# Hybrid encoder block on one core: the last column group of the second token tile in two halves, its sums between the first tile's output pieces

## The chip, the cores and the metric

The kernel runs on one core of a Trainium2 chip. Five engines work side by side, each with its own queue, and meet through semaphores: TensorE (PE, matmuls; its weight loads are listed as PEld), VectorE (DVE), ScalarE (ACT), GpSimd (POOL) and SyncE (SP, which issues most DMA transfers). Matmuls write PSUM, 128 partitions with eight banks of 512 floats each; everything else lives in SBUF. The metric is the time of one execution on the device in microseconds; lower is better. An execution that is profiled also gives a span, from the first to the last instruction.

## The reference, cut to what matters

One layer (DEPTH is 1) on 256 tokens of 2048 features, all in float32:

```python
def reference(x, ...):
    u = _rms_norm(x, norm_mix_pre)
    mix = hybrid_mixer(u, ...)            # three branches, gates, w_out
    x = x + _rms_norm(mix, norm_mix_post)
    hdn = jnp.square(jax.nn.relu(_rms_norm(x, norm_mlp_pre) @ w_mlp_up))
    return x + _rms_norm(hdn @ w_mlp_down, norm_mlp_post)

def _rms_norm(x, gain):
    return x * lax.rsqrt(jnp.mean(x * x, axis=-1, keepdims=True) + 1e-6) * gain
```

The end of the kernel is the last line of the reference: the product with w_mlp_down (8192 x 2048), its norm over the 2048 features of each token, the gain and the residual. A token's norm needs all of its 2048 columns, so no column of the output can be written before the last column of the product is summed.

## The kernel before, in words

The 256 tokens are two tiles of 128 (`tt` 0 and 1). Float32 products run as products of rounded parts: a weight tile is read as `raw`, ScalarE rounds it into `whi`, VectorE subtracts to get `wlo`, and TensorE multiplies the activations' high and low parts by `whi` and their high part by `wlo`, all summed in one PSUM bank. The weights come as one stream of rows of 128 x 1024, 512 KB a piece, on SP's queue.

Most of w_mlp_down has been multiplied and added into `ys[0]` and `ys[1]` (one per token tile, 128 x 2048) when the stretch of the diff begins. What is left are the last 8 blocks of 128 hidden features (`hp`), for four column groups of 512 (`g` 0 to 3). The generator `tok` does one column group: for every pair of blocks it takes a weight tile and multiplies both token tiles by it, each into its own bank (`ps[0]`, `ps[1]`, from the pool `pg` of four banks). `lag` is the number of trailing weight tiles for which the two token tiles are parted: the first tile is finished with them, `ps[0]` is handed out, then the second is multiplied by the same tiles and `ps[1]` follows. For `g` 3 the lag is 4, all of them: 24 matmuls for the first tile, then 24 for the second (four weight tiles, two blocks each, three products a block). The three last weight tiles get buffers of their own (`spare`), so that they can stay.

As a bank is handed out, the loop at line 1574 does for that token tile: the sum into `ys` on VectorE (line 1578); the square on ScalarE, with the sum over the 512 columns accumulated into `ss4[:, tt, g]` (line 1579); for `g` 3 the mean over all columns by an activation with a bias (`rstd_of`, line 1151) and the power of -0.5 on GpSimd (line 1152), which gives `r4`; the multiplication by the gain `g4[g]` on VectorE, in place (line 1582). After `g` 2 `rstd_of` has added the sums of the first three groups and epsilon into `sum4`. Last, in five pieces of 512, 512, 512, 256 and 256 columns, VectorE writes x1 + ys * r4 into `x1` (line 1588), and each piece is sent to the output, the second and fourth on ScalarE's queue and the others on SP's (line 1589).

The end up to this stretch has its order written out by hand for TensorE, ScalarE and VectorE only in places (`tc.manual_schedule`); elsewhere, and in the loop at 1574, a scheduler orders the engines' queues by the instructions' dependencies. Instructions of one engine run in the order of its queue.

## Time and profile before

| what | value |
|---|---|
| median of three runs | 1502.87 us (1501.86 to 1506.22) |
| the profiled execution's own time | 1503.08 us |
| its span | 1501.2 us, 22710 instructions |
| mean granted TensorE clock | 0.998 |
| TensorE busy from 200 to 1100 us | 100% |
| TensorE busy from 1300 to 1400 us | 99.3% |
| HBM read and written | 279.24 MB and 2.10 MB |
| the output's ten transfers, issue to landing | 2.5 to 3.3 us each |
| GpSimd's work after the last accumulating transfer | two powers of one column |

Rows of a timeline give the start and the length in microseconds, the engine, the line of the kernel, the operation, the tile written and those read, their shapes, the count of instructions merged into the row, and in brackets the idle time before it with what ended it. Rows of groups end with the busy time, the mean of one instruction in ns, and the idle time before them. In the rows of windows the numbers after the length of the window are busy microseconds and counts of PE, PEld, DVE, ACT and POOL, then the granted clock, the share of the DMA engines and GB/s. A DMA queue's row has its packets, MB and share of 16 engines.

### The profile page before, as it was taken

The page shows a single profiled execution, that of the slowest core. Times are in us where ns is not written, and L with a number is a line of the kernel's source. Part 1 is how long each engine was busy: PE and PEld are TensorE (multiplying, and loading weights), DVE is VectorE, ACT ScalarE, POOL GpSimd, SP SyncE. Part 2 cuts the span into 40 slices and gives each one's busy share as a digit, 9 for nine tenths or more (in the row PEclk, how much of TensorE's full clock was granted, in tenths as well). Part 3 has the DMA queues.
Part 4 walks back from the last instruction along what each step waited for, and adds up shares of the span by engine and source line. Part 5 has one row for each costly group of instructions (what it writes and reads, how often), then busy time and mean ns, then how long its engine had stood idle before and what let it go on. Part 6 is the DMA issues. An engine that isn't in the chain of part 4 may idle for free.

```text
span 1501.2 us, 22710 instructions
## 1 busy us (share of the span) xinstructions
PE 1487.4 (99%) x8384; PEld 1250.2 (83%) x8384; DVE 1205.8 (80%) x1677; ACT 933.3 (62%) x1431; POOL 94.7 (6%) x151
## 2 busy tenths in 40 slices
PE   9999999999999999999999999999999999999997
PEld 8888888887788887788888888888888888888886
DVE  7965779895687895476557688998999989999996
ACT  7665677555765445564545676776666666767663
POOL 0011003000002000000000000000000000000000
PEclk9999999999999999999999999999999999999999
DMA  8655445454555455455774868889898888989874
GB/s 288 202 154 175 154 161 172 152 182 154 164 174 174 156 183 183 131 174 191 243 235 153 267 181 256 250 223 260 259 257 256 229 268 250 262 259 262 255 218 148
DMA packets 107055, 312.19 MB, mean 208 GB/s; under 512 B 12352, under 2 KB 14400, under 8 KB 106944
## 3 DMA queue, kind: packets, MB, share of 16 engines
q1 hardware_dynamic: 96336, 279.35, 57.0%
q0 software_dynamic: 8064, 29.36, 10.3%
q10 hardware_dynamic: 2544, 2.03, 0.5%
q8 instruction: 66, 1.08, 0.3%
q14 instruction: 45, 0.37, 0.1%
HBM read 279.24 MB, written 2.10 MB: 187 GB/s over the span
## 4 chain that ended last, share of the span: by engine, by line
PE 96%; DMA 1%; DVE 1%; issue 1%; ACT 1%; SPq 0%; POOLq 0%; DVEq 0%; POOL 0%; ACTq 0%
PE gps L235 28%; PE gps L191 22%; PE gps L195 12%; PE gps L220 7%; PE mps L1434 3%; PE mps L1436 3%; PE mps L1435 3%; PE gps L1436 2%; PE gps L1434 2%; PE gps L1435 2%; PE gps L197 2%; PE gps L359 1%; DMA raw<-raw 1%; PE mps L840 1%; DMA raw<-in_wst_dram 1%
## 5 line engine op out<-in xcount | busy, mean ns | idle before, releaser
L175 DVE TENSOR_TENSOR wlo<-raw,whi 128x1024 fp32r<-128x1024 f32 x570 | 691.3, 1223 | 151.0 <-ACT whi L173 140.6
L173 ACT ACTIVATE whi<-raw 128x1024 fp32r<-128x1024 f32 x570 | 597.6, 1057 | 253.7 <-PE gps L235 71.8
L191 PE MATMUL gps<-pk,whi 128*128 128x512 f32 x1460 | 370.6, 392 | 0.5 <-DVE tmp L1352 0.2
L191 PEld LDWEIGHTS gps<-pk,whi 128*128 128x128 f32 x1460 | 270.4, 188 | 56.2 <-DVE tmp L1352 1.2
L235 PE MATMUL gps<-whi,pk 128*128 128x512 f32 x1004 | 253.5, 392 | 0.0
L195 PEld LDWEIGHTS gps<-pk,wlo 128*128 128x128 f32 x1561 | 212.7, 190 | 15.2 <-DVE wlo L175 0.3
L235 PEld LDWEIGHTS gps<-whi,pk 128*128 128x128 f32 x1004 | 186.5, 188 | 40.1 <-issue 1.0
L195 PE MATMUL gps<-pk,wlo 128*128 128x256 f32 x1561 | 218.0, 282 | 0.0
L235 PE MATMUL gps<-wlo,pk 128*128 128x512 f32 x502 | 138.2, 392 | 0.0
L235 PEld LDWEIGHTS gps<-wlo,pk 128*128 128x128 f32 x502 | 93.2, 188 | 19.6 <-issue 0.2
L1434 PE MATMUL mps<-whi,fm 128*128 128x512 f32 x224 | 88.6, 396 | 1.8 <-ACT whi L173 1.7
L1351 ACT ACTIVATE tmp<-gps 128x256 f32<-128x256 f32 x64 | 24.6, 385 | 102.8 <-PE gps L197 100.9
L1435 PE MATMUL mps<-whi,fm 128*128 128x512 f32 x224 | 87.7, 392 | 0.0
L1436 PE MATMUL mps<-wlo,fm 128*128 128x512 f32 x224 | 87.4, 390 | 0.0
L1414 POOL DMA_DIRECT2D raw<-raw x56 | 48.8, 872 | 572.7 <-DVE raw L1411 299.1
L1411 DVE TENSOR_TENSOR raw<-raw,raw 128x1024 f32<-128x1024 f32 x56 | 68.3, 1220 | 0.8
L1434 PE MATMUL gps<-whi,fm 128*128 128x512 f32 x168 | 65.8, 392 | 0.0
L1436 PE MATMUL gps<-wlo,fm 128*128 128x512 f32 x168 | 65.7, 391 | 0.0
L1435 PE MATMUL gps<-whi,fm 128*128 128x512 f32 x168 | 65.5, 390 | 0.0
L220 PE MATMUL gps<-whi,pk 128*128 128x512 f32 x224 | 60.7, 393 | 0.0
L1434 PEld LDWEIGHTS mps<-whi,fm 128*128 128x128 f32 x224 | 42.4, 189 | 10.0 <-ACT whi L173 3.9
L1436 PEld LDWEIGHTS mps<-wlo,fm 128*128 128x128 f32 x224 | 42.1, 188 | 9.4
(359 smaller groups left out, 1738.3 us busy)
## 6 DMA issues: line engine op xcount, KB each, us to landing
raw<-in_wst_dram SPq DMA_DIRECT2D x510, 512.0 KB, 4.4
raw<-raw POOLq DMA_DIRECT2D x56, 512.0 KB, 8.5
x<-in_xt_dram SPq DMA_DIRECT2D x8, 256.0 KB, 5.3
x<-in_x_dram SPq DMA_DIRECT2D x8, 256.0 KB, 5.3
raw<-in_wst_dram SPq DMA_DIRECT2D x6, 256.0 KB, 5.0
pk<-in_wst_dram SPq DMA_DIRECT2D x6, 256.0 KB, 5.2
g<-in_gains_dram SPq DMA_DIRECT2D x4, 256.0 KB, 4.8
pk<-in_gains_dram SPq DMA_DIRECT2D x4, 256.0 KB, 6.7
```

The lines of the kernel that those rows point to most:

```text
L173: A.activation(hi, raw, AF.Copy)
L175: low = lambda: V.tensor_tensor(lo, raw, hi.bitcast(F32), ALU.subtract)
L191: PE.matmul(ps, hi[:, i * 128:i * 128 + 128], pks[i], start=first and i == 0, stop=False)
L195: PE.matmul(ps[:, 0:T], lo[:, i * 128:i * 128 + 128], pks[i][:, 0:T], start=False, stop=False)
L197: PE.matmul(ps, hi[:, (n - 1) * 128:n * 128], pks[n - 1], start=False, stop=True)
L220: PE.matmul(ps[tt], pks[k][:, c:c + 128], w[:, (k - k0) * 512:(k - k0) * 512 + 512], start=k == 0 and part == 0 and w is hl[0], stop=w is ...
L235: PE.matmul(ps[tt], pks[k][:, c:c + 128], w[:, (k - k0) * 512:(k - k0) * 512 + 512], start=k == 0 and part == 0 and w is hl[0], stop=False)
L1411: V.tensor_tensor(R[d, a], R[d, a], R[d, b], ALU.add)
L1414: G.dma_start(out=R[d, a], in_=R[d, b], accum_op=ALU.add)
L1434: PE.matmul(Q[f], a, w, start=d == d0 and i == 0, stop=False)
L1435: PE.matmul(Q[f], b, w, start=False, stop=False)
L1436: PE.matmul(Q[f], a, wl, start=False, stop=d == dn and i == 1)
```

## The change

- `tok` takes a list of column ranges for the second token tile. With `((0, 256), (256, 512))` the matmuls of the kept weight tiles run first for columns 0 to 255, into `ps[1]`, and then again for columns 256 to 511, into a further bank (`more[0]`); each is handed out when done. All 24 matmuls of 512 columns become 48 of 256, and each still loads its own weights.
- The squares are taken of values scaled by 2048 to the power -0.5, so the accumulated sums are means at once.
- For `g` 3 the sum goes to a new tile (`yl[tt]`, 512 columns and one more, in buffers of the pool of `fm`) instead of `ys`, and the product with the gain is written from there into `ys`. It no longer overwrites what the square reads.
- The mean of the other columns plus epsilon enters through the additional column: GpSimd writes the root of it times 2048 there (`root`), and the square of 513 (or 257) columns adds it. The activation of line 1151 is gone for these two tiles; the power of -0.5 (`factor`) reads the accumulated column itself.
- The pieces become 256, 512, 512, 512 and 256 columns, the second and fourth on ScalarE's queue.
- The order on ScalarE, VectorE and GpSimd is written out: the first half's sum of the second tile stands after two pieces of the first tile, `sum4[1]` and its root after the third, the first half's product with the gain and the second half's sum after the fifth.
- `last4`, 128 x 2 x 2 floats, is a further tile in `cpool`, the first pool in SBUF. By the addresses that the two programs give their tiles, every pool in SBUF behind it starts 32 bytes higher: the weight tiles started at multiples of 256 bytes and now start 32 bytes past them.

The names in the rows below: `gps` are PSUM banks, `kw`, `whi` and `wlo` weight tiles, `fm` the blocks `hp` (on TensorE) or the new tiles `yl` and `spent` (elsewhere), `y` the tiles `ys`, `pk` the gain, `rs` the factor of a token tile, `x` the tile `x1`, `last` and `ss` the accumulated squares.

On TensorE, at the start of the second token tile of the last column group; before:

```order
L220 MATMUL gps_14411<-whi_14380,fm_13461 128x512 x2
L220 MATMUL gps_14411<-whi_14380,fm_13464 128x512 x2
L220 MATMUL gps_14411<-wlo_14381,fm_13461 128x512
L220 MATMUL gps_14411<-wlo_14381,fm_13464 128x512
L220 MATMUL gps_14411<-kw_14414,fm_13912 128x512 x2
L220 MATMUL gps_14411<-kw_14414,fm_13915 128x512 x2
```

and now, where the first half ends and the second begins:

```order
L220 MATMUL gps_14418<-kw_14445,fm_14133 128x256 x2
L220 MATMUL gps_14418<-kw_14445,fm_14136 128x256 x2
L220 MATMUL gps_14418<-kw_14446,fm_14133 128x256
L220 MATMUL gps_14418<-kw_14446,fm_14136 128x256
L220 MATMUL gps_14461<-whi_14381,fm_13462 128x256 x2
L220 MATMUL gps_14461<-whi_14381,fm_13465 128x256 x2
L220 MATMUL gps_14461<-wlo_14382,fm_13462 128x256
L220 MATMUL gps_14461<-wlo_14382,fm_13465 128x256
```

The 24 matmuls into one bank have become 24 into one and 24 into another, each of half as many columns. All rows of TensorE ahead of them are the same as before.

On VectorE, from the sum of the first token tile to the end; before:

```order
L1578 TENSOR_TENSOR y_8764<-y_8764,gps_14410 128x512
L1582 TENSOR_TENSOR y_8764<-y_8764,pk_14153 128x512
L1588 SCALAR_TENSOR_TENSOR x_1389_7403<-y_8764,rs_14457,x_1389_7403 128x512 x3
L1588 SCALAR_TENSOR_TENSOR x_1389_7403<-y_8764,rs_14457,x_1389_7403 128x256 x2
L1578 TENSOR_TENSOR y_8765<-y_8765,gps_14411 128x512
L1582 TENSOR_TENSOR y_8765<-y_8765,pk_14153 128x512
L1588 SCALAR_TENSOR_TENSOR x_1390_7404<-y_8765,rs_14498,x_1390_7404 128x512 x3
L1588 SCALAR_TENSOR_TENSOR x_1390_7404<-y_8765,rs_14498,x_1390_7404 128x256 x2
```

and now, from the first tile's second piece to the second tile's first:

```order
L1618 SCALAR_TENSOR_TENSOR x_1389_7404<-y_8765,rs_14515,x_1389_7404 128x512
L1604 TENSOR_TENSOR fm_14412<-y_8766,gps_14418 128x256
L1618 SCALAR_TENSOR_TENSOR x_1389_7404<-y_8765,rs_14515,x_1389_7404 128x512
L1632 TENSOR_TENSOR ssum_14408<-ssum_14408,last_14414 128x1
L1598 TENSOR_SCALAR ssum_14408<-ssum_14408 128x1
L1618 SCALAR_TENSOR_TENSOR x_1389_7404<-y_8765,rs_14515,x_1389_7404 128x512
L1618 SCALAR_TENSOR_TENSOR x_1389_7404<-y_8765,rs_14515,x_1389_7404 128x256
L1607 TENSOR_TENSOR y_8766<-fm_14412,pk_14154 128x256
L1604 TENSOR_TENSOR fm_14412<-y_8766,gps_14461 128x256
L1607 TENSOR_TENSOR y_8766<-fm_14412,pk_14154 128x256
L1618 SCALAR_TENSOR_TENSOR x_1390_7405<-y_8766,rs_14536,x_1390_7405 128x256
```

Five instructions of the second tile (its first half's sum and product with the gain, two of one column, and the second half's sum) stand among or right after the pieces of the first, where there was one sum.

On ScalarE, the same stretch; before:

```order
L1579 ACTIVATE junk_14455,ss_8157<-y_8764 128x512
L1151 ACTIVATE rs_14457<-ss_8157,ssum_14394 128x1
L1589 DMA out_dram<-x_1389_7403 128x512
L1589 DMA out_dram<-x_1389_7403 128x256
L1579 ACTIVATE junk_14496,ss_8157<-y_8765 128x512
L1151 ACTIVATE rs_14498<-ss_8157,ssum_14407 128x1
L1589 DMA out_dram<-x_1390_7404 128x512
L1589 DMA out_dram<-x_1390_7404 128x256
```

and now:

```order
L1606 ACTIVATE fm_14413,last_14414<-fm_14411 128x513
L1619 DMA out_dram<-x_1389_7404 128x512
L1606 ACTIVATE fm_14413,last_14414<-fm_14412 128x256
L1619 DMA out_dram<-x_1389_7404 128x512
L1606 ACTIVATE fm_14413,last_14414<-fm_14412 128x257
L1619 DMA out_dram<-x_1390_7405 128x512 x2
```

The two activations of one column are gone, the second tile has two squares, and an output issue of the first tile stands ahead of each of them.

The diff, cut to its core:

```diff
-    def tok(pks, lag=1, mid=()):
+    def tok(pks, lag=1, mid=(), cols=((0, 512),)):
...
-        def prod(hl, k0, tt):
+        def prod(hl, k0, tt, a=0, b=512):
...
-                        PE.matmul(ps[tt], pks[k][:, c:c + 128], w[:, (k - k0) * 512:(k - k0) * 512 + 512],
+                        PE.matmul((ps[tt] if a == 0 else more[0])[:, a:b], pks[k][:, c:c + 128], w[:, (k - k0) * 512 + a:(k - k0) * 512 + b],
...
-        for i, (hl, k0) in enumerate(kept):
-            prod(hl, k0, 1)
-            tick()
-            if i < len(mid):
-                mid[i]()
-        yield ps[1]
+        more = [gps()] if len(cols) > 1 else []
+        for a, b in cols:
+            for i, (hl, k0) in enumerate(kept):
+                prod(hl, k0, 1, a, b)
+                tick()
+                if i < len(mid):
+                    mid[i]()
+            yield ps[1] if a == 0 else more[0]
...
-    for i, v in enumerate((CE, GN_EPS, -0.5)):
+    for i, v in enumerate((CE, GN_EPS, -0.5, 0.5)):
...
+    yl, spent = [line() for _ in range(2)], line()
+    last4 = cpool.tile([128, 2, 2], F32, name="last4")
+
+    def root(tt):
+
+        V.tensor_scalar(sum4[tt], sum4[tt], float(D), None, ALU.mult)
+        G.tensor_tensor(yl[tt][:, 512:513], sum4[tt], cst[:, 3:4], ALU.pow)
+
+    def close(tt, a, b, ps, whole):
+
+        t = yl[tt]
+        V.tensor_tensor(t[:, a:b], ys[tt][:, 1536 + a:1536 + b], ps[:, a:b], ALU.add)
+        q = last4[:, tt, whole:whole + 1]
+        A.activation(spent[:, a:b + whole], t[:, a:b + whole], AF.Square, scale=rows, accum_out=q)
+        return lambda: V.tensor_tensor(ys[tt][:, 1536 + a:1536 + b], t[:, a:b], g4[3][:, a:b], ALU.mult)
+
+    def factor(tt):
+
+        r4 = cpool.tile([128, 1], F32, name=nm("rs"))
+        G.tensor_tensor(r4, last4[:, tt, 1:2], cst[:, 2:3], ALU.pow)
+        return r4
+
+    def piece(tt, r4, i):
+        c, w = ((0, 256), (256, 512), (768, 512), (1280, 512), (1792, 256))[i]
+        cs = slice(c, c + w)
+        V.scalar_tensor_tensor(x1[tt][:, cs], ys[tt][:, cs], r4, x1[tt][:, cs], ALU.mult, ALU.add)
+        (nc.scalar if i % 2 else nc.sync).dma_start(out=out[tt * 128:tt * 128 + 128, cs], in_=x1[tt][:, cs])
+
+    ends = tok(hp, 4, (), ((0, 256), (256, 512)))
+    root(0)
+    banks = [next(ends) for _ in range(3)]
+    manual = tc.manual_schedule(engines={mybir.EngineType.Activation, mybir.EngineType.DVE, mybir.EngineType.Pool})
+    manual.__enter__()
+    close(0, 0, 512, banks[0], 1)()
+    r4 = factor(0)
+    for i in range(2):
+        piece(0, r4, i)
+    gained = close(1, 0, 256, banks[1], 0)
+    piece(0, r4, 2)
+    V.tensor_tensor(sum4[1], sum4[1], last4[:, 1, 0:1], ALU.add)
+    root(1)
+    for i in range(3, 5):
+        piece(0, r4, i)
+    gained()
+    gained = close(1, 256, 512, banks[2], 1)
+    gained()
+    r4 = factor(1)
+    for i in range(5):
+        piece(1, r4, i)
```

More of the change, by code (lines that the diff above doesn't have):

```diff
@@ L1573, in hybrid_block @@
     home[0] = spare
-    for g in range(4):
+    rows = D ** -0.5
+    for g in range(3):
         gs = slice(512 * g, 512 * g + 512)
-        for tt, ps in enumerate(tok(hp, 4 if g == 3 else 1)):
+        for tt, ps in enumerate(tok(hp)):
             yv = ys[tt][:, gs]
             V.tensor_tensor(yv, yv, ps, ALU.add)
-            A.activation(junk(), yv, AF.Square, accum_out=ss4[:, tt, g:g + 1])
-            if g == 3:
-                r4 = rstd_of(ss4[:, tt, :], None, sum4[tt])
+            A.activation(junk(), yv, AF.Square, scale=rows, accum_out=ss4[:, tt, g:g + 1])
@@ L1582, in hybrid_block @@
             V.tensor_tensor(yv, yv, g4[g], ALU.mult)
             if g == 2:
[L1584 to L1590 removed]
+                e = cpool.tile([128, 1], F32, name=nm("ssum"))
@@ new lines, in hybrid_block @@
+    manual.__enter__()
[15 more added lines that the diff above has]
+        piece(1, r4, i)
+    manual.__exit__(None, None, None)
```

12 lines of the change are left out of this document (5 added, 7 removed).

## The prediction, made before the changed kernel ran

> **What bounds the kernel now.** I read the page's table of engines first, then the chain of waits of the last 30 us, then their timeline, because the diff moves no instruction before that.
>
> ```profile
> PE 1487.4 (99%) x8384; PEld 1250.2 (83%) x8384; DVE 1205.8 (80%) x1677; ACT 933.3 (62%) x1431; POOL 94.7 (6%) x151
> 1477.87 8.18 PE gps L220 x36
> 1486.07 0.70 DVE y L1578
> ...
> 1486.85 0.73 ACT junk L1579 x2
> ...
> 1487.60 0.30 ACT rs L1151
> ...
> 1487.98 0.74 POOL rs L1152
> ```
>
> TensorE is busy for 99% of the span, so in the body nothing counts but matmuls. At the end the chain leaves TensorE (the list is its part from 1477.87 on): sum, square, mean, power, pieces. It does so once per token tile. The list follows the first tile's round; the second's is in the timeline (start, length, instruction):
>
> ```profile
> 1485.87 1.07 PE L220 MATMUL gps<-whi,fm 128*128 128x512 f32 x4
> 1487.23 4.24 PE L220 MATMUL gps<-kw,fm 128*128 128x512 f32 x18
> 1487.60 0.69 DVE L1582 TENSOR_TENSOR y<-y,pk 128x512 f32<-128x512 f32 x1 [0.85 <-ACT junk L1579]
> 1488.75 2.87 DVE L1588 SCALAR_TENSOR_TENSOR x<-y,rs,x 128x512 f32<-128x512 f32 x5 [0.46 <-POOL rs L1152]
> 1491.54 0.68 DVE L1578 TENSOR_TENSOR y<-y,gps 128x512 f32<-128x512 f32 x1
> 1492.25 0.63 ACT L1579 ACTIVATE junk<-y 128x512 f32<-128x512 f32 x1 [4.35 <-DVE y L1578]
> 1492.79 0.19 ACT L1579 ACTIVATION_READ_ACCUMULATOR junk<-y 128x1 f32 x1
> 1493.01 0.29 ACT L1151 ACTIVATE rs<-ss,ssum 128x1 f32<-128x1 f32 x1
> 1493.38 0.73 POOL L1152 TENSOR_TENSOR rs<-rs,cst 128x1 f32<-128x1 f32 x1 [4.66 <-ACT rs L1151]
> 1494.14 2.87 DVE L1588 SCALAR_TENSOR_TENSOR x<-y,rs,x 128x512 f32<-128x512 f32 x5 [0.44 <-POOL rs L1152]
> ```
>
> The last matmul ends at 1487.23 + 4.24 = 1491.47. VectorE has just finished the first tile's five pieces (1488.75 + 2.87 = 1491.62, the next one overlapping their tail), so TensorE and VectorE arrive together. From there to the end of the span (1501.2) are 9.7 us: sum 0.7, square and its reading 0.7, mean 0.3, power 0.73, handovers, pieces 2.87, and about 4.2 for the last output transfer and the closing waits. No edit of this stretch can win more than a part of 9.7 us, or 0.65% of the time.
>
> **The change part by part.** *Matmuls in halves.* The second tile's 24 matmuls (4 + 2 + 18) of 512 columns become 48 of 256. The spacing of the old ones is (1487.23 - 1485.87) / 6 = 0.227 us. For 256 columns, each with a fresh weight load, there is a row:
>
> ```profile
> 1445.22 1.12 PE L195 MATMUL gps<-pk,wlo 128*128 128x256 f32 x8
> L195 PE MATMUL gps<-pk,wlo 128*128 128x256 f32 x1561 | 218.0, 282 | 0.0
> L195 PEld LDWEIGHTS gps<-pk,wlo 128*128 128x128 f32 x1561 | 212.7, 190 | 15.2 <-DVE wlo L175 0.3
> ```
>
> Eight of them take 1.12 us, one lasts 0.28, so they start (1.12 - 0.28) / 7 = 0.12 us apart. The first half ends at 1485.87 + 23 x 0.12 + 0.28 = 1488.91, the second at 1485.87 + 47 x 0.12 + 0.28 = 1491.79: TensorE is done 0.32 us later than now. On its own that is +0.32 on the path.
>
> *The mean leaves ScalarE.* Mean and epsilon now enter as a 513th (257th) column whose square is the bias, so the 0.30 us activation goes and the power waits for the read accumulator alone. Gone per tile: from the end of the read (1486.85 + 0.73 = 1487.58) to the power's start (1487.98), 0.40 us, less one handover of 0.08 (1487.90 to 1487.98): 0.32. The column itself is made by a power on GpSimd, and the last square waits for it as well as for its sum; behind that square on ScalarE stand two output issues of the second tile, which nobody needs before. For the second tile this power follows the one-column instructions (below, about 2.4 us after the first piece) and takes at most 0.73, so it is done by 3.2 us, over 1 us before the square can start at 3.85 + 0.42.
>
> *The multiplication by the gain no longer waits for the square* and moves from beside the power to ahead of it. That may shorten the power:
>
> ```profile
> L1152 POOL TENSOR_TENSOR rs<-rs,cst x4: 555/642/736, 806.2 to 1493.4; 128x1 f32<-128x1 f32 x4
> 806.24 0.56 POOL L1152 TENSOR_TENSOR rs<-rs,cst 128x1 f32<-128x1 f32 x1 [316.97 <-ACT rs L1151]
> 805.87 0.69 DVE L1246 TENSOR_TENSOR mg<-gps,g 128x512 f32<-128x512 f32 x1 [3.40 <-ACT junk L1243]
> ```
>
> The same power took 0.56 beside a VectorE instruction that reads PSUM and SBUF, and 0.73 twice beside L1582, which reads two SBUF tiles. If that is the cause, each power drops by 0.18; if not, by nothing. The nearest row, a power with no such neighbour, is 0.56, so I take most of it.
>
> *VectorE's order.* First tile: sum at 1486.07 as now, square read by 1487.57, power from 1487.66 to 1488.22 (or 1488.40), pieces from 1488.25 (or 1488.43) instead of 1488.75. Then between the pieces come the first half's sum, two one-column instructions and the first half's gain. Their prices:
>
> ```profile
> L1588 DVE SCALAR_TENSOR_TENSOR x<-y,rs,x 128x512 f32<-128x512 f32 x6 | 4.2, 746 | 0.9 <-POOL rs L1152 0.9
> L1588 DVE SCALAR_TENSOR_TENSOR x<-y,rs,x 128x256 f32<-128x256 f32 x4 | 1.7, 476 | 0.0
> 1396.83 0.42 DVE L1352 TENSOR_TENSOR tmp<-gps,tmp 128x256 f32<-128x256 f32 x1
> 1397.17 1.22 DVE L1411 TENSOR_TENSOR raw<-raw,raw 128x1024 f32<-128x1024 f32 x1
> L1366 DVE TENSOR_TENSOR eps<-eps 128x1 f32<-128x1 f32 x2 | 0.3, 158 | 0.1
> 1387.97 0.41 ACT L1353 ACTIVATE tmp<-tmp 128x256 f32<-128x256 f32 x1
> 1388.27 1.05 ACT L173 ACTIVATE whi<-raw 128x1024 fp32r<-128x1024 f32 x1
> ```
>
> Five pieces last 3 x 0.746 + 2 x 0.476 = 3.19 but took 2.87, so each overlaps the next by 0.08: spacings 0.67 and 0.40. A 256-column sum is followed after 0.34. Piece, piece, half sum, piece: 0.40 + 0.67 + 0.34 + 0.67 = 2.08. The two one-column instructions, the second waiting for the first, about 2 x 0.16 + 0.04 = 0.36; the squares they wait for (half sum done 1.07 + 0.42 = 1.49 after the start, 0.08 of handover, 0.30 + 0.19 on ScalarE) are there at 2.06, in time. Then piece, piece, gain: 0.67 + 0.40 + 0.34 = 1.41. VectorE comes to the second half's sum 3.85 us after the first piece, at 1492.10 (or 1492.28), although TensorE was done at 1491.79: it is VectorE, 0.25 to 0.42 late, that sets this point, and the 0.32 us lost on TensorE lies under it. ScalarE's queue also holds two output issues ahead of its squares, both released by then; SP's holds only pieces in order.
>
> Then: sum 0.42, handover 0.08 (as 1486.77 to 1486.85 now), square 0.30 (257 columns: 0.32), reading 0.19, handover 0.08, power 0.56 (or 0.73), 0.03. From 1492.10 this gives 1493.78, at the other end 1492.28 + 1.85 = 1494.13, against 1494.14 now. **The second tile's pieces start 0.35 us earlier or at the same time.** Their own length is the same, 2.87.
>
> *Output.* Ten transfers remain ten; the first piece is now 128 KB and the fourth 256 KB.
>
> ```profile
> DMA to landing us min/median/max: 2.5/3.0/3.3
> 1497.00:1498.00 1.00, 0.00 (x0) 0.00 (x0) 0.01 (x1) 0.00 (x0) 0.00 (x0) 0.50 1.05 313
> 1498.00:1499.00 1.00, 0.00 (x0) 0.00 (x0) 0.00 (x0) 0.00 (x0) 0.00 (x0) 0.50 0.89 264
> ```
>
> The DMA engines (share 1.05, then 0.89) are still full after the last piece is computed, so what stands behind the last issue counts: 128 KB more there, at 313 KB per us, is at most 0.4 us, and nothing where the earlier, smaller first piece has let the queue run ahead. The two ends of everything: -0.35 and 0, plus 0 to 0.4: **-0.35 to +0.4 us**. I take -0.2, since the price of the power is better founded than the full backlog. The profiled execution was 1503.08 (span 1501.2 and 1.9 around it), which gives 1502.9; it lies 0.2 above the median of 1502.87, so the median should be about **1502.7**.
>
> **The rivals.** *A, the matmuls' price goes with their number, not their columns.* If a weight load (0.19) and the stream of 256 columns (0.12) stood one after the other, 48 would cost 14.9 us instead of 5.4: +9.4 and 1512 us. It decides from a spacing of 0.21. Against it: the L195 rows, eight pairs at 0.12. The Trainium skill (TensorE: Matmul & The Clock Gate, Part 3, "The mechanism") says that a weight load overlaps running matmuls only where the row group differs, which would be this rival. By that rule the load cannot hide here; the trace's 0.12 does not agree with it.
>
> *B, the move of the buffers slows the body.* One new tile in the first SBUF pool moves every pool behind it by 32 bytes, so all weight rows land 32 bytes past the boundary on which they now start. In the second half of the program transfers are dense:
>
> ```profile
> 1300.00:1400.00 100.00, 99.29 (x497) 83.35 (x496) 96.69 (x112) 70.15 (x96) 8.70 (x10) 1.00 0.91 263
> q10 hardware_dynamic: 384, 0.16, 9.6%
> q1 hardware_dynamic: 96336, 279.35, 57.0%
> L1086 DVE TENSOR_TENSOR m<-m,th 128x512 f32<-128x512 f32 x16 | 10.9, 684 | 0.2
> L1441 DVE TENSOR_TENSOR y<-y,junk 128x512 f32<-128x512 f32 x22 | 15.1, 684 | 0.1
> ```
>
> The DMA share there is 0.91. Were each packet 17% dearer, it would pass 1 (1.06), and 550 us of this stage would stretch by about 6% where dense, half that on average: some +16 us, 1519. It decides from 10% on. Against it: the tile gup starts at such an odd address already, and its queue (window 634 to 640) moved 384 packets of some 420 bytes in 9.6% of 16 engines x 6 us, 24 ns each. The weights' queue (the page's row of q1) took 0.57 x 16 x 1501 us for 279 MB, 49 ns per KB, or 21 ns for as many bytes, and short rows are the dearer ones. VectorE takes 684 ns with the odd tile th and without. Below 10% it costs nothing, as TensorE hides it.
>
> *C, faster than I say:* if VectorE kept up with TensorE (the half sum at 1491.86), another 0.25, and with a last transfer that finds an empty queue 0.3: -0.9 us, 1502.0. The order speaks against it: three VectorE instructions stand between. *D, the halves save nothing* and TensorE's 0.32 comes through: if VectorE reached the second sum at 1491.86 but the power stayed at 0.73 and the mean's 0.32 were eaten by the column's power on GpSimd, +0.4: 1503.3.
>
> **How the numbers follow.** About 0.3%, 4.5 us, is what a measurement of this kernel can tell from no change; C and D are inside it like the forecast. Forecast with C and D 0.80; A 0.03; B 0.08, with 0.04 for a move that happens to help the body; 0.05 for runs that stray (the three of before lie 4.4 us apart), 0.03 of it fast and 0.02 slow. Faster 0.07, same 0.80, slower 0.13. The range takes the sum's ends, 1502.0 to 1503.3, and the spread of medians around them, most of it upward as in the runs shown: 1500.9 to 1505.2; A and B lie outside with about 0.1.
>
> **What would show it.** The timeline after should have 256-column L220 matmuls 0.12 us apart (0.21 or more: A); a power near 0.56; the second half's sum starting at 1492.1 to 1492.3 with VectorE, not TensorE, ahead of it; the second tile's first piece at 1493.8 to 1494.1. Everything before 1485 should stand where it did to within a microsecond; if it moved by several, B (or its opposite) is at work and the forecast is wrong.

## The result and the profile after

The changed kernel took **1501.43 us** (median of 22 runs, 1500.53 to 1503.12); the kernel before, on the same chip in the same session, 1504.03 (22 runs, 1501.86 to 1507.43). The ratio is 0.9986, 95% interval 0.998 to 0.9992. Forecast were 1502.7 us, a range from 1500.9 to 1505.2, and "within 0.3%" with a chance of 0.80. The time is inside both. But the gain is about 2 us by the ratio, and the sum had -0.2.

The timeline of the changed kernel, from the start of the second token tile's matmuls:

```profile
1484.89 0.64 PE L220 MATMUL gps<-whi,fm 128*128 128x256 f32 x4
1485.09 0.69 DVE L1604 TENSOR_TENSOR fm<-y,gps 128x512 f32<-128x512 f32 x1 [1.52 <-PE gps L220]
1485.60 2.32 PE L220 MATMUL gps<-kw,fm 128*128 128x256 f32 x18
1485.81 0.69 DVE L1607 TENSOR_TENSOR y<-fm,pk 128x512 f32<-128x512 f32 x1
...
1486.41 0.19 ACT L1606 ACTIVATION_READ_ACCUMULATOR fm<-fm 128x1 f32 x1
1486.67 0.55 POOL L1612 TENSOR_TENSOR rs<-last,cst 128x1 f32<-128x1 f32 x1 [2.52 <-ACT fm L1606]
1487.25 1.15 DVE L1618 SCALAR_TENSOR_TENSOR x<-y,rs,x 128x256 f32<-128x256 f32 x2 [0.75 <-POOL rs L1612]
...
1488.48 2.32 PE L220 MATMUL gps<-kw,fm 128*128 128x256 f32 x18
...
1489.70 1.14 DVE L1618 SCALAR_TENSOR_TENSOR x<-y,rs,x 128x512 f32<-128x512 f32 x2
1489.93 0.92 POOL L1599 TENSOR_TENSOR fm<-ssum,cst 128x1 f32<-128x1 f32 x1 [2.71 <-DVE ssum L1598]
...
1490.76 0.42 DVE L1607 TENSOR_TENSOR y<-fm,pk 128x256 f32<-128x256 f32 x1
1491.09 0.42 DVE L1604 TENSOR_TENSOR fm<-y,gps 128x256 f32<-128x256 f32 x1
...
1491.60 0.42 ACT L1606 ACTIVATE fm<-fm 128x257 f32<-128x257 f32 x1 [2.20 <-DVE fm L1604]
1491.93 0.19 ACT L1606 ACTIVATION_READ_ACCUMULATOR fm<-fm 128x1 f32 x1
1492.19 0.55 POOL L1612 TENSOR_TENSOR rs<-last,cst 128x1 f32<-128x1 f32 x1 [1.34 <-ACT fm L1606]
1492.77 2.87 DVE L1618 SCALAR_TENSOR_TENSOR x<-y,rs,x 128x256 f32<-128x256 f32 x5 [0.81 <-POOL rs L1612]
```

The last matmul ends at 1488.48 + 2.32 = 1490.80. The second half's sum starts at 1491.09, 0.29 us later: VectorE, not TensorE, is awaited there, as forecast. The two profiled executions are best laid beside each other from the first tile's last sum on, since from there on only the end counts (before 1486.07, after 1485.09). The second tile's first piece starts 8.07 us behind that sum before and 7.69 now, 0.39 sooner (8.074 and 7.686 before rounding). From that sum to the end of the span it was 15.15 us, and now it is 14.06: **1.09 us less**. So 0.7 us of this gain lies behind the start of the pieces, where the prediction had expected nothing or a loss.

The output transfers of the second tile, in the view of the DMA issues cut to this stretch (line, queue, count, size, median us from issue to landing), before:

```profile
out_dram<-x SPq DMA_DIRECT2D x2, 256.0 KB, 2.7
out_dram<-x ACTq DMA_DIRECT2D x1, 256.0 KB, 2.7
out_dram<-x ACTq DMA_DIRECT2D x1, 128.0 KB, 3.3
out_dram<-x SPq DMA_DIRECT2D x1, 128.0 KB, 3.0
```

and after, with the windows in which they run (the last two columns are the share of the DMA engines and GB/s):

```profile
out_dram<-x ACTq DMA_DIRECT2D x2, 256.0 KB, 2.2
out_dram<-x SPq DMA_DIRECT2D x2, 128.0 KB, 2.1
out_dram<-x SPq DMA_DIRECT2D x1, 256.0 KB, 2.2
```

```profile
1495.00:1496.00 1.00, 0.00 (x0) 0.00 (x0) 0.64 (x2) 0.00 (x0) 0.00 (x0) 0.50 0.99 377
1496.00:1497.00 1.00, 0.00 (x0) 0.00 (x0) 0.00 (x0) 0.00 (x0) 0.00 (x0) 0.50 0.99 370
```

Each transfer lands about half a microsecond sooner, and full engines (share 0.99) move 370 to 377 GB/s, where the rows of before quoted in the prediction show 313 at a share of 1.05 and 264 at 0.89. The row just ahead of those two had more:

```profile
1496.00:1497.00 1.00, 0.00 (x0) 0.00 (x0) 1.00 (x3) 0.00 (x0) 0.00 (x0) 0.55 1.02 363
```

The engines are as busy and move more. That was the riddle of this case.

The body ahead of 1485 moved too, by -1.0 us (the sum at 1485.09 instead of 1486.07). It is in one place; a row of the waits of TensorE in 1190 to 1225 us of before, and the window in which it lies, before and after (busy PE is the first number behind the length):

```profile
PE mps L1434 <- ACT whi L173: 1.0, 1, 1.0
```

```profile
1100.00:1200.00 100.00, 98.63 (x503) 83.43 (x502) 93.11 (x112) 68.26 (x96) 8.70 (x10) 1.00 0.87 246
```

```profile
1100.00:1200.00 100.00, 99.96 (x515) 85.36 (x514) 95.30 (x116) 69.56 (x97) 8.70 (x10) 1.00 0.84 238
```

TensorE's busy time gains 1.33 us there and loses 0.26 in the next 100 us (99.73 before, 99.47 after); nothing else differs by as much. Whether the change did that, by the 32 bytes that it moves the weight tiles, is the first question of the experiments.

### The profile page after: what moved, and what is told of

Read it like the earlier page. It is cut to its first block, busy times and chain, and to the rows that moved or that the text cites. A ratio compares the mean times of both kernels' runs of the same rounds, so it can differ in the third digit from the quotient of the medians.

```text
span 1499.1 us, 22770 instructions
## 1 busy us (share of the span) xinstructions
PE 1488.0 (99%) x8408; PEld 1252.0 (84%) x8408; DVE 1206.6 (80%) x1682; ACT 934.0 (62%) x1431; POOL 95.8 (6%) x154
## 4 chain that ended last, share of the span: by engine, by line
PE 97%; DVE 1%; ACT 1%; DMA 0%; issue 0%; SPq 0%; POOL 0%; DVEq 0%; POOLq 0%; ACTq 0%
PE gps L235 28%; PE gps L191 23%; PE gps L195 13%; PE gps L220 7%; PE mps L1436 3%; PE mps L1437 3%; PE mps L1438 3%; PE gps L1438 2%; PE gps L1436 2%; PE gps L1437 2%; PE gps L197 2%; PE gps L361 1%; PE mps L842 1%; PE gps L1225 1%; DMA x<-in_xt_dram 0%
```

## The experiments

Two theories stood against each other for the difference of the two medians, and the expectations call them by letter. **T**, the tail: the change shortens the end alone, by some 1.1 us, and what the body does differs from run to run. **P**, the place: the move of all buffers by 32 bytes also changes the waits of the body. Later runs take the 1.1 us apart. In this table "piece", "issue", "data" and "end" are the start of the second tile's first piece, the last output issue, the last byte written and the end of the span, all in us behind the start of the first tile's last sum in the same trace. The two last columns are the mean duration in ns of that tile's output packets of 2 KB and of 1 KB, from the packet records of the trace. The ratio is against the kernel before, run beside it.

| run | median us (runs) | ratio, 95% interval | piece | issue | data | end | 2 KB | 1 KB |
|---|---|---|---|---|---|---|---|---|
| before | | | 8.07 | 10.97 | 13.37 | 15.15 | 97 | 58 |
| after | 1501.43 (22) | 0.9986, 0.998 to 0.9992 | 7.69 | 10.58 | 12.29 | 14.06 | 85 | 45 |
| after, again (a1_again) | 1502.14 (11) | 0.9993, 0.9983 to 1.0003 | 7.68 | 10.57 | 12.28 | 14.03 | 85 | 45 |
| before, buffers moved (s1_shift32) | 1502.55 (11) | 0.9994, 0.9986 to 1.0003 | 8.08 | 10.97 | 13.41 | 15.15 | 97 | 58 |
| the same again (s1_again) | 1502.63 (11) | 0.9998, 0.9989 to 1.0007 | 8.07 | 10.97 | 13.36 | 15.11 | 97 | 57 |
| after, buffers not moved (s2_unshifted) | 1502.00 (11) | 0.9993, 0.9985 to 1.0002 | 7.68 | 10.57 | 12.19 | 13.98 | 84 | 46 |
| after, no halves (t1_whole) | 1501.33 (11) | 0.9988, 0.9979 to 0.9997 | 7.63 | 10.52 | 12.22 | 13.99 | 85 | 45 |
| after, old pieces (t2_old_pieces) | 1502.68 (11) | 0.9993, 0.9984 to 1.0002 | 7.69 | 10.58 | 12.97 | 14.74 | 97 | 58 |
| before, new pieces (p1_pieces) | 1504.12 (1) | | 8.08 | 10.97 | 12.59 | 14.37 | 84 | 46 |
| before, old pieces turned (p5_turned) | 1501.25 (1) | | 8.07 | 10.97 | 12.52 | 14.27 | 84 | 46 |
| before, new pieces turned, in another order (p6_turned) | 1502.95 (1) | | 8.08 | 10.97 | 13.19 | 14.87 | 95 | 57 |
| after, no halves, gain beside the power (m1_beside) | 1501.60 (1) | | 7.69 | 10.58 | 12.29 | 14.04 | 85 | 45 |
| after, sum ahead of the gain (f1_order) | 1501.06 (11) | 0.9986, 0.9977 to 0.9995 | 7.43 | 10.33 | 12.04 | 13.78 | 86 | 46 |
| that, last piece on other engines (f2_three_engines) | 1502.24 (10) | 0.9997, 0.9987 to 1.0007 | 7.44 | 10.41 | 12.10 | 14.60 | 84 | 46 |

The kernel before, run beside them, had medians of 1503.15, 1502.92 and 1502.71 us in the three later sessions.

### The 32 bytes: s1_shift32, s1_again, s2_unshifted, a1_again

The kernel before with every SBUF pool moved as the change moves it, and no instruction added:

```diff
-    cst = cpool.tile([128, 4], F32, name="cst")
+    cst = cpool.tile([128, 12], F32, name="cst")
```

> The kernel before with the tile of constants widened from 4 to 12 columns: no instruction is added, every SBUF pool behind it starts 32 bytes higher, as in the changed kernel. Theory P (the 32 bytes win what the tail does not): about 1.7 us faster than before (0.9989), with fewer runs above 1504. Theory T (only the tail wins, the rest is the luck of runs): equal to before within 0.7 us (1.000). The rival B of the prediction, turned round, is P.

The changed kernel with the pools where they were before:

```diff
-    cst = cpool.tile([128, 4], F32, name="cst")
+    cst = cpool.tile([128, 8], F32, name="cst")
...
-    last4 = cpool.tile([128, 2, 2], F32, name="last4")
+    last4 = cst[:, 4:8].rearrange("p (a b) -> p a b", a=2)
```

> The changed kernel with last4 placed in spare columns of the tile of constants, so that all pools stand where they stood before. Theory P: 0.9 us faster than before (0.9994), the runs spread over 1501 to 1506 like those of before. Theory T: as fast as the changed kernel, 2 to 2.6 us (0.9985).

Both were measured beside each other; in the next session the moved kernel before and the changed kernel were run once more.

> The kernel before with all pools 32 bytes higher, once more. Theory T: ratio 1.000, 15.1 us behind the first tile's sum. Theory P: 0.9990 or below. Together with the first 11 runs this should bound what the move is worth to about 0.6 us.

> The changed kernel once more, beside the kernel before on one chip. So far its span was 2.1 us shorter, of which 1.1 lie behind the first token tile's last sum (14.0 us from there to the end against 15.1) and 1.0 in the body, while runs gave a ratio of 0.9986. Theory T (only the end differs): 1.1 us faster, 0.9993, and 14.0 us again behind the first tile's sum. Theory P (32 bytes): 2 to 2.6 us faster, 0.9985.

The move alone gives 0.9994 and 0.9998, neither apart from 1, and an end of 15.15 and 15.11 us like the 15.15 of before. The changed kernel without the move gives 0.9993, the same ratio as the changed kernel when it was measured again. The first pair of runs did not decide: s1_shift32 lies between P's 0.9989 and T's 1.000, and s2_unshifted came out at P's 0.9994 and not at T's 0.9985. The second pair gives what T expected (0.9998 and 0.9993), and so do the ends of all four traces. What is left open is a small move of the body: the interval of s1_again reaches down to 0.9989, 1.7 us. How far the body wanders by itself is seen in programs that are alike up to the first tile's last sum: in before, p1_pieces, p5_turned and p6_turned it starts at 1486.07, 1487.97, 1485.20 and 1486.21. A spread of 2.8 us between equal bodies leaves no cause to be sought for the -1.0 in a single pair of traces. Over all traces the sum starts at 1485.4 on average in the nine with the move (1484.8 to 1486.2) and at 1486.1 in the five without (1485.2 to 1488.0); the ranges overlap, so some tenths of a microsecond are neither shown nor excluded. What the change itself brings is the 1.09 us at the end, 0.07%. That would be a ratio of 0.9993: it is the second ratio of the changed kernel, and lies just outside the first one's interval (0.998 to 0.9992). That the rest of the first is chance is likely by this, but not shown.

### One part undone: t1_whole, t2_old_pieces, p1_pieces

The changed kernel without the halves of the second token tile:

```diff
-    ends = tok(hp, 4, (), ((0, 256), (256, 512)))
+    ends = tok(hp, 4)
     root(0)
-    banks = [next(ends) for _ in range(3)]
+    root(1)
+    banks = [next(ends) for _ in range(2)]
...
-    for i in range(2):
-        piece(0, r4, i)
-    gained = close(1, 0, 256, banks[1], 0)
-    piece(0, r4, 2)
-    V.tensor_tensor(sum4[1], sum4[1], last4[:, 1, 0:1], ALU.add)
-    root(1)
-    for i in range(3, 5):
+    for i in range(5):
         piece(0, r4, i)
-    gained()
-    gained = close(1, 256, 512, banks[2], 1)
-    gained()
+    close(1, 0, 512, banks[1], 1)()
```

> The changed kernel with the second tile's last group whole again (24 matmuls of 512 columns into one bank, one sum, one square, after the first tile's five pieces). If the halves pay for nothing because VectorE comes late to the second sum: pieces of the second tile start within 0.2 us of the changed kernel's place relative to the last matmul of the first tile (7.9 us after it). If the halves are what wins: 0.3 to 0.6 us later.

Its end is 13.99 us, that of the changed kernel 14.06: **the halves are worth nothing** as they stand. The second sum comes sooner without them, and takes longer, as does its square; here is its second tile:

```profile
1491.01 0.69 DVE L1604 TENSOR_TENSOR fm<-y,gps 128x512 f32<-128x512 f32 x1 [0.41 <-PE gps L220]
...
1492.61 0.55 POOL L1612 TENSOR_TENSOR rs<-last,cst 128x1 f32<-128x1 f32 x1 [4.91 <-ACT fm L1606]
1493.19 1.15 DVE L1618 SCALAR_TENSOR_TENSOR x<-y,rs,x 128x256 f32<-128x256 f32 x2 [0.78 <-POOL rs L1612]
```

From the sum to the piece it is 2.18 us here and 1.68 in the changed kernel (1491.09 to 1492.77); the half microsecond saved there is what VectorE lost by coming later (5.44 us behind the first tile's sum here, 6.00 there).

Then the changed kernel with the sizes of pieces and the queues of before:

```diff
-        c, w = ((0, 256), (256, 512), (768, 512), (1280, 512), (1792, 256))[i]
+        c, w = ((0, 512), (512, 512), (1024, 512), (1536, 256), (1792, 256))[i]
```

> The changed kernel with the old pieces, 512, 512, 512, 256, 256 columns. Theory: the earlier first transfer and the larger packets near the end shorten the closing transfer by 0.7 us, so here the last transfer lands 3.0 us after its issue again, and the run is 0.7 us slower than the changed kernel. Rival: the transfer's gain came from something else (the order on VectorE, the move by 32 bytes): landing stays at 2.3 us.

and the kernel before with the new ones and nothing else of the change:

```diff
-                for c, w in (0, 512), (512, 512), (1024, 512), (1536, 256), (1792, 256):
+                for c, w in (0, 256), (256, 512), (768, 512), (1280, 512), (1792, 256):
...
-                    (nc.scalar if c == 512 or w == 256 and c == 1536 else nc.sync).dma_start(
+                    (nc.scalar if c in (256, 1280) else nc.sync).dma_start(
```

> The kernel before with the new pieces alone (256, 512, 512, 512, 256, the second and fourth on ScalarE's queue). If the 0.7 us of the closing transfer comes from the pieces alone: 14.4 us behind the first tile's sum instead of 15.1, the last transfer landing 2.3 us after its issue. If it needs the other edits: 15.1 and 3.0.

Undone, the pieces cost 0.68 us of the end (14.74 against 14.06); done alone, they bring 0.78 (14.37 against 15.15), although the first piece and the last issue stand where they stood, at 8.08 and 10.97. What differs is the time from the last issue to the last byte, 2.40 us with the old pieces and 1.62 with the new ones. The packet records show where it goes: both sets have 384 packets of 2 KB and 256 of 1 KB per tile, but with the old pieces the mean packet takes 97 and 58 ns, with the new ones 84 and 46. In the second tile of before the first transfer runs at 84 ns throughout; from the second on single packets take up to 204.

### Sizes or addresses: p5_turned, p6_turned

The new pieces differ from the old in two ways: in size and time, and in the columns at which they begin. With the old ones every row of 2 KB begins on a 2 KB boundary (columns 0, 512, 1024), with the new ones 1 KB past it (256, 768, 1280). The kernel before with its old sizes, queues and times, its instructions on every engine in the old order, and only the columns turned by 256:

```diff
-                for c, w in (0, 512), (512, 512), (1024, 512), (1536, 256), (1792, 256):
+                for i, (c, w) in enumerate(((256, 512), (768, 512), (1280, 512), (1792, 256), (0, 256))):
...
-                    (nc.scalar if c == 512 or w == 256 and c == 1536 else nc.sync).dma_start(
+                    (nc.scalar if i % 2 else nc.sync).dma_start(
```

> Kernel before, with its pieces in their old sizes and order of sizes (512, 512, 512, 256, 256), on the old queues at the old times; only the columns that they take are moved by 256: 256 to 767, 768 to 1279, 1280 to 1791, 1792 to 2047, 0 to 255. So only the addresses of the rows read and written change, by 1 KB. Known: with the old pieces the 2 KB packets of the output took 97 ns on average and the 1 KB packets 58, from the second transfer of a tile on; with the new pieces 84 and 46, the same number of each. Theory A (address: rows of 2 KB that begin on 2 KB boundaries hold each other up, rows that begin 1 KB past one do not): 84 and 46 ns here too, the last data 0.5 to 0.7 us sooner behind the last issue than the 2.40 of before, the stretch from the first tile's last sum to the end of the span 14.5 to 14.7 us instead of 15.13. Theory F (the small first piece lets the queue run ahead, and the small piece at the end is alone): packets stay at 97 and 58, stretch 15.0 to 15.2.

and p1_pieces with its sizes kept and the columns turned back onto the boundaries:

```diff
-                for c, w in (0, 256), (256, 512), (768, 512), (1280, 512), (1792, 256):
+                for i, (c, w) in enumerate(((1792, 256), (0, 512), (512, 512), (1024, 512), (1536, 256))):
...
-                    (nc.scalar if c in (256, 1280) else nc.sync).dma_start(
+                    (nc.scalar if i % 2 else nc.sync).dma_start(
```

> Kernel before with the new sizes of pieces on the new queues (256, 512, 512, 512, 256), but taking the columns 1792 to 2047, 0 to 511, 512 to 1023, 1024 to 1535, 1536 to 1791, so that rows of 2 KB begin on 2 KB boundaries as before. With the new sizes at their new places this stretch was 14.33 us, 0.80 less than the 15.13 of before. Theory A (address): packets of 97 and 58 ns, the early start alone is left, stretch 14.7 to 15.1. Theory F (sizes and the early start): 84 and 46 ns, 14.2 to 14.4.

The transfers of p5_turned, old sizes off the boundaries, by their landings and by windows:

```profile
out_dram<-x SPq DMA_DIRECT2D x2, 256.0 KB, 2.1
out_dram<-x ACTq DMA_DIRECT2D x1, 256.0 KB, 2.1
out_dram<-x ACTq DMA_DIRECT2D x1, 128.0 KB, 2.2
out_dram<-x SPq DMA_DIRECT2D x1, 128.0 KB, 2.2
```

```profile
1495.00:1496.00 1.00, 0.00 (x0) 0.00 (x0) 1.00 (x3) 0.00 (x0) 0.00 (x0) 0.50 0.99 385
1496.00:1497.00 1.00, 0.00 (x0) 0.00 (x0) 0.14 (x1) 0.00 (x0) 0.00 (x0) 0.50 1.03 389
```

The packets are as theory A expected (84 and 46 ns), and the end is 14.27, still earlier than its 14.5 to 14.7.

In p6_turned the sizes did not come in the order that the edit lists. The loop leaves the order to the scheduler, and columns 0 to 511 went first, on ScalarE's queue, and the small piece second. The group of pieces is named by its first one, which has 512 columns here (256 in p1_pieces), and ScalarE's queue issues before SP's:

```profile
1494.29 2.87 DVE L1588 SCALAR_TENSOR_TENSOR x<-y,rs,x 128x512 f32<-128x512 f32 x5 [0.44 <-POOL rs L1152]
1495.07 2.06 ACTq L1589 DMA_DIRECT2D out_dram<-x  x2
1495.47 2.05 SPq L1589 DMA_DIRECT2D out_dram<-x  x3
```

The first issue stands 8.86 us behind the first tile's sum, where it stood in before (8.85). So this run has a third order (512, 256, 512, 512, 256) and no early start; it shows rows on the boundaries in another order, and not theory F's small first piece. Its transfers by windows:

```profile
1496.00:1497.00 1.00, 0.00 (x0) 0.00 (x0) 1.00 (x3) 0.00 (x0) 0.00 (x0) 0.50 1.07 372
1497.00:1498.00 1.00, 0.00 (x0) 0.00 (x0) 0.16 (x1) 0.00 (x0) 0.00 (x0) 0.50 1.10 355
1498.00:1499.00 1.00, 0.00 (x0) 0.00 (x0) 0.00 (x0) 0.00 (x0) 0.00 (x0) 0.50 0.91 269
```

The slow packets follow the addresses and not the sizes: on the boundaries a share of 1.10 moves 355 GB/s, off them 1.03 moves 389. The end in us:

| | rows begin on 2 KB boundaries | 1 KB past them |
|---|---|---|
| sizes and queues of before | 15.15 (before) | 14.27 (p5_turned) |
| new sizes | 14.87 (p6_turned, small piece second) | 14.37 (p1_pieces, small piece first) |

**Turning the columns of the old pieces by 256 gives 0.88 us**, more than all of the new sizes at their places. Before and p5_turned differ in nothing else, and the reading by address rests on this pair; theory F's small first piece is not needed for fast packets. Off the boundaries the new sizes bring nothing more (14.37 against 14.27); what the 0.28 us of p6_turned come from, with 95 and 57 ns, was not separated. p5_turned moves a row's place in SBUF and in the output alike, so which of the two addresses counts stays open. An exact boundary in SBUF it is not: in s1_shift32, s1_again and t2_old_pieces the tiles in SBUF stand 32 bytes higher, and the packets take 97 and 57 to 58 ns as before.

### The power and its neighbour: m1_beside

The prediction laid the slow powers to a multiplication of two SBUF tiles beside them. To put it back, t1_whole got a copy of one column behind each square, so that the gain starts when the power does:

```diff
-    close(0, 0, 512, banks[0], 1)()
+    gained = close(0, 0, 512, banks[0], 1)
+    V.tensor_copy(last4[:, 0, 0:1], last4[:, 0, 1:2])
+    gained()
...
-    close(1, 0, 512, banks[1], 1)()
+    gained = close(1, 0, 512, banks[1], 1)
+    V.tensor_copy(last4[:, 1, 0:1], last4[:, 1, 1:2])
+    gained()
```

> Changed kernel without the halves (one sum, square and gain for the second tile's last column group, which measured a power of 0.55 us and a stretch of 14.03 us), and with a copy of one column on VectorE after each of the two squares that must wait for the square, so that the multiplication by the gain again stands beside the power instead of ahead of it. If the power is slower because VectorE multiplies two SBUF tiles beside it: both powers of the factor 0.73 us instead of 0.55, the second tile's pieces 0.2 us or more later after its sum, stretch 14.2 to 14.5. If the column that replaced the activation made the power shorter: 0.55 as without the copy.

```profile
1492.78 0.15 DVE L1634 COPY last<-last 128x1 f32<-128x1 f32 x1 [0.87 <-ACT fm L1606]
1492.83 0.55 POOL L1612 TENSOR_TENSOR rs<-last,cst 128x1 f32<-128x1 f32 x1 [4.91 <-ACT fm L1606]
1492.85 0.70 DVE L1607 TENSOR_TENSOR y<-fm,pk 128x512 f32<-128x512 f32 x1
```

The power takes 0.55 us as without the copy, and the end is 14.04 us, not 14.2 to 14.5: the gain stands beside the power and does not slow it. It started 0.02 us behind it. The expectation tied this outcome to the missing activation, but that is not the cause either: the power at 806.24 in before, quoted in the prediction, follows such an activation and took 0.56. In before the power (1487.98) met a multiplication that had been running since 1487.60 and had 0.31 us left, and took 0.18 more; in the changed kernel the root at 1489.93 met a piece that had been running since 1489.70 and had about half a microsecond left, and took 0.92, 0.37 more. A third case is in t2_old_pieces, where the root met a piece of 256 columns with 0.25 us left and took 0.66, 0.11 more:

```profile
1491.05 0.48 DVE L1618 SCALAR_TENSOR_TENSOR x<-y,rs,x 128x256 f32<-128x256 f32 x1
1491.28 0.66 POOL L1599 TENSOR_TENSOR fm<-ssum,cst 128x1 f32<-128x1 f32 x1 [2.98 <-DVE ssum L1598]
```

In all three the power loses what is left of the running instruction, less 0.13 to 0.15 us. The rows fit a wait for its end, and not a slowdown by a neighbour. The Trainium skill (SBUF — State Buffer, "Who interferes with whom") says that VectorE with two SBUF inputs and a GpSimd instruction that reads SBUF shut each other out, and that the order of issue decides which of them waits. The powers here agree. That VectorE is held up when it comes second does not show here: the gain behind the power took 0.70 us, and 0.69 alone. Behind a longer GpSimd instruction it does show, in f2_three_engines below.

### Two steps further: f1_order, f2_three_engines

In the changed kernel VectorE multiplies the first half by the gain (1490.76) ahead of the second half's sum, which ScalarE and GpSimd wait for. Nobody waits for that product before the pieces:

```diff
-    gained()
-    gained = close(1, 256, 512, banks[2], 1)
-    gained()
+    later_half = close(1, 256, 512, banks[2], 1)
+    gained()
+    later_half()
```

> The changed kernel with the first half's multiplication by the gain moved behind the second half's sum. If VectorE's lateness is what keeps the halves from paying: the second half's sum starts at TensorE's end, 0.25 to 0.3 us earlier, and 13.7 us remain behind the first tile's sum. If something else limits: 14.0.

```profile
1491.07 0.42 DVE L1604 TENSOR_TENSOR fm<-y,gps 128x256 f32<-128x256 f32 x1
1491.41 0.75 DVE L1607 TENSOR_TENSOR y<-fm,pk 128x256 f32<-128x256 f32 x2
...
1492.17 0.55 POOL L1612 TENSOR_TENSOR rs<-last,cst 128x1 f32<-128x1 f32 x1 [1.09 <-ACT fm L1606]
1492.75 1.81 DVE L1618 SCALAR_TENSOR_TENSOR x<-y,rs,x 128x256 f32<-128x256 f32 x3 [0.59 <-POOL rs L1612]
```

The sum follows the last matmul (1491.03) by 0.04 us, and both gains run under the square. The pieces start 7.43 us behind the first tile's sum, 0.26 sooner, and the end is 13.78, 0.28 less. With this order the halves win 0.21 us over t1_whole (13.99). Its median, 1501.06, is the lowest of all, with the ratio 0.9986; beside it the changed kernel had 0.9993. The intervals overlap, so the trace carries this gain and the times do not contradict it.

Last, with this order, the second tile's last piece on other engines, while VectorE does four:

```diff
     r4 = factor(1)
+    cs = slice(1792, 2048)
+    A.activation(spent[:, 0:256], ys[1][:, cs], AF.Copy, scale=r4)
+    piece(1, r4, 0)
+    G.tensor_tensor(x1[1][:, cs], spent[:, 0:256], x1[1][:, cs], ALU.add)
+    nc.sync.dma_start(out=out[128:256, cs], in_=x1[1][:, cs])
-    for i in range(5):
+    for i in range(1, 4):
         piece(1, r4, i)
```

> Changed kernel with the second half's sum ahead of the first half's gain, and the second tile's last piece of 256 columns computed on ScalarE (times the factor) and GpSimd (plus x1) while VectorE does the other four. If VectorE's 2.87 us of pieces set the end: last issue up to 0.4 us sooner, time 0.2 to 0.4 us below that with the order alone. If the transfers set it (DMA share 0.99 in the last two microseconds), the end stays where it was to within 0.1 us. If GpSimd is held up by VectorE beside it (a power beside the pieces took 0.92 us instead of 0.55), its piece comes last and the end is later by 0.3 us or more.

```profile
1492.27 2.94 DVE L1618 SCALAR_TENSOR_TENSOR x<-y,rs,x 128x256 f32<-128x256 f32 x4 [0.60 <-POOL rs L1612]
1492.85 1.15 POOL L1643 TENSOR_TENSOR x<-fm,x 128x256 f32<-128x256 f32 x1 [0.62 <-ACT fm L1641]
1493.33 1.21 DVE L1618 SCALAR_TENSOR_TENSOR x<-y,rs,x 128x512 f32<-128x512 f32 x1
```

Four pieces on VectorE now take 2.94 us, where five took 2.87, and GpSimd's addition beside them takes 1.15. The last row, one of the four by itself, shows why: a piece of 512 columns that starts while the addition runs takes 1.21 us instead of 0.75. The last issue comes 0.08 us later than in f1_order and the last byte 0.06 later. The end is 14.60, 0.82 later, though the last byte is not: the time from it to the end of the span is 2.50 us here and 1.74 there. The instructions of the closing, which are listed by the line of the kernel's call, show what it waits for; first in f2_three_engines, then in f1_order (durations in ns, then the first and last start in us):

```profile
L1768 POOLq DRAIN  x3: 34/102/5841, 1492.8 to 1499.2; - x3
L1768 POOLq EVENT_SEMAPHORE  x4: 17/17/17, 1498.7 to 1499.3; - x4
```

```profile
L1763 POOLq DRAIN  x3: 34/93/5246, 1492.1 to 1498.8; - x3
L1763 POOLq EVENT_SEMAPHORE  x4: 17/17/17, 1498.4 to 1499.0; - x4
```

The first DRAIN of GpSimd's queue starts just ahead of its last instruction and ends 4.66 us after that instruction, in each of the fourteen traces. GpSimd's closing semaphores follow about 1.0 us behind the last byte in thirteen of them, 0.8 to 1.7 us after this drain is done. In f2_three_engines the last instruction is the addition, which ends at 1494.00: the drain lasts to 1498.65, 1.7 us beyond the last byte at 1496.93, and the semaphores follow it by 0.04 us. So none of the three expected limits set this end: the last byte came no sooner, and GpSimd's piece was issued at 1494.02, ahead of two others. It was GpSimd's drain behind a late instruction, and what the drain does in these 4.66 us the traces do not show. The ratio is 0.9997 (0.9987 to 1.0007): of the gain nothing is left that could be told from none.

## Why the prediction came out, step by step

*Matmuls in halves.* Right: the rows of 2.32 us for 18 give a spacing of (2.32 - 0.28) / 17 = 0.12, and the last matmul ends 5.71 us behind the first tile's sum, against 5.72 forecast (1491.79 - 1486.07). Rival A is out.

*The mean leaves ScalarE.* Right: from the end of the read to the power it is 0.07 us in both tiles (1486.60 to 1486.67, 1492.12 to 1492.19), where it was 0.40.

*The power.* The size is right, 0.55 instead of 0.73, and the condition, "if that is the cause", was only half of it: m1_beside shows that a neighbour does no harm when it starts behind the power. That the gain moved ahead is what helped, since it is done by then (1486.50, the power starts at 1486.67). The column's power, which was to take "at most 0.73", took 0.92; it was still done in time.

*VectorE's order.* Right: it comes to the second half's sum 3.84 us after the first piece (3.85 forecast), 0.29 us behind TensorE (0.25 to 0.42). The second tile's pieces start 7.69 us behind the first tile's sum; the forecast, counted from there, was 7.71 to 8.06, so it lies 0.02 before the early end. The table's f1_order shows that VectorE's lateness was not a price of the halves but of one misplaced instruction: the prediction took the order as given.

*Output.* Here the prediction failed, by the step "128 KB more there, at 313 KB per us, is at most 0.4 us, and nothing where the earlier, smaller first piece has let the queue run ahead". It took the pace of the transfers in before, 313 and 264 GB/s, for the pace of full engines, and so could find only a loss. It was the pace of slow packets. With rows off the 2 KB boundaries full engines move 370 GB/s and more, and the term is -0.7 us. The sign came out of a quantity that the prediction did not look at, the addresses of the rows; the share of 1.05 beside a falling GB/s was in the quoted rows, and the row ahead of them had 363 GB/s at 1.02.

*The sum.* -0.39 for the start of the pieces (forecast -0.35 to 0) and -0.70 for the output (0 to +0.4) make the 1.09 us of the end. The sum's ends were -0.35 and +0.4, so the end lies outside them: the time came out inside its range because the range was made wide for the spread of runs, and that is luck. What the first median shows beyond that belongs to no term: the body, which was to stand "to within a microsecond", stood 1.0 us sooner. Rival B, priced at 16 us, is out by s1_shift32 and s1_again; of its opposite they show nothing, but they leave room for up to 1.7 us. Rival C (-0.9) came nearest in size; of its two reasons the one, VectorE keeping up, did not come about, and the other, a shorter last transfer, did, though not from an empty queue; D is out, since each of its three conditions is: VectorE is late, the power is short, and the column's root, though 0.92 us long, is done at 1490.85, before the square at 1491.60 needs it.

## What to carry to other kernels

When DMA engines are full and the GB/s fall, look at the duration of single packets before taking that pace for a limit: here the last of the same bytes in the same sizes landed 0.85 us sooner when each row began 1 KB past a 2 KB boundary instead of on it. On an engine that is late at a handover, put what others wait for ahead of what only it needs; a half that was finished early was worth nothing until that was done. Before giving GpSimd work near the end, look at how long its queue takes to close: in f2_three_engines the span ended 5.4 us after GpSimd's last instruction, and this closing set the end. And with a body that wanders by microseconds between equal programs, measure an edit of the end from an event just ahead of it in the same trace.

## What the runs showed of the chip that was not expected

- Output rows of 2 KB, 8 KB apart, on 2 KB boundaries: the first transfer of a tile runs at 84 to 86 ns a packet, and from the second on packets take up to 204 ns in the second tile of before (means 97 and 57 to 58 ns for 2 KB and 1 KB in four traces with the old pieces, 95 and 57 in p6_turned). Turned by 1 KB, the means are 84 to 86 and 45 to 46 in nine traces. It shows also in transfers of 1 KB rows that are under way with slow ones or right behind them.
- A power of one column on GpSimd takes 0.55 us beside a VectorE instruction of two SBUF tiles that starts 0.02 us later, 0.66 behind one with 0.25 us left, 0.73 behind one with 0.31, and 0.92 behind one with about half a microsecond. A piece of 512 columns on VectorE that starts beside a GpSimd addition of two SBUF tiles takes 1.21 us instead of 0.75.
- GpSimd's first DRAIN of the closing ends 4.66 us after its last instruction in all fourteen traces. In f2_three_engines that is what the end waits for, and the time from the last byte to the end of the span is 2.50 us; in the others it is 1.7 to 1.8.
